# First output product of a two-layer encoder: the loads of the last two gates on ScalarE's queue, and the residual of one quarter loaded into its row tile ahead

## The chip, the cores and the metric

The kernel runs on one core of one Trainium2 chip. The metric is the time of one execution on the device in microseconds (us), taken as the median of several runs.

A core has five engines that each work through their own instructions in order: TensorE (PE, matrix products), VectorE (DVE), ScalarE (ACT), GpSimd (POOL) and SyncE (SP). They wait for one another through semaphores. SP issues most DMA transfers; POOL issues some, among them all that add to what is in the target (accumulate); ScalarE issues one small one at the start and six stores of the output at the end.

## The reference

Two encoder layers over `x` (512 tokens x 1024) and 256 memory tokens. Each layer projects its normed input to mixer heads, memory queries and a gate, and ends with a gated output projection that is added to the residual:

```python
for i in range(DEPTH):                    # DEPTH = 2
    h = rmsnorm(x, norm_g[i])
    mem_h = rmsnorm(mem, mem_norm_g[i])
    proj = jnp.einsum('bsd,de->bse', h, w_in)          # w_in_a in layer 0, w_in_b in layer 1
    ...                                                # split into mixer heads, q_mem and gate
    o = concat(mixer(...), memory_attention(q_mem, mem_h, ...))   # 512 x 1536: 8 mixer heads, 4 memory heads
    x = x + (o * silu(gate)) @ w_out[i]                # w_out: 1536 x 1024
```

The part that matters here is the last line in the first layer (called layer A below).

## The kernel before

**Products.** Every projection is computed in float32 by splitting both factors into a high and a low part and adding three products: high x high (`mm_early`, L177), low activation x high weight (L178) and high activation x low weight (`mm_late`, L181). On top of that, large products are taken as 2 x 2 blocks with seven block products instead of eight (the Strassen-Winograd scheme). The block products are called 11, 12, S1, S2, S3, S4 and 22; the four quarters of the result are called 11, 12, 21 and 22, where the first digit is the half of the tokens (rows) and the second the half of the output columns.

**Weights.** One weight tile is 128 x 1024 (512 KB). SP loads it (`wl`, L259), ScalarE rounds it to the high part (`wh`, L321), DVE subtracts for the low part (`wo`, L331). Some tiles are sums of weight blocks that POOL's accumulating DMAs build (L295, L305). TensorE uses one tile in one "run" of eight early and four late matmuls of 128 x 512.

**Order.** The program is written out in Python and nothing reorders it later. A `Driver` counts slots (one per run): generators such as `fold` or `gate.ev` do one step in a slot and `yield n` to come back n slots later. So the text of a step, its yields and the slot in which it started decide where its instructions stand in each engine's order.

**Gates of layer A.** The last chunks of layer A are `b`, `m` and `a` (`A_ORDER = "01234567bma"`): the gates of heads 4 to 7 (g = 2), of the memory heads (g = 0) and of heads 0 to 3 (g = 1). `gate.ev` takes a quarter of a gate's product, `load()` fetches the head outputs `od` from DRAM into a tile `og` (256 KB, L863, on SP), ScalarE takes tanh (L886), DVE makes the SiLU and multiplies by `og` (L878) into `yf`. `prep_y` makes the seven activation blocks `YW` from `yf` (casts L919, subtractions L920, differences such as L942 and L947), `prep_l` those of gate `b`, called `YL` (L994, L997).

**Output product.** `out_proj` calls `s_chunk` with `late=YL`. The seven block products come in the order `PRODUCTS_3` (11, S3, 12, S1, S2, S4, 22), each in three runs, the third with `YL`. Behind each stands one step of `after`, done for each of two token rows `u`: hold z, hold s3, add_11, hold s5, fold s2, add 12, add 21. The pieces of the result lie in four "row tiles" `acc` (128 tokens x 1024 each; rows 0 and 1 hold the quarters 11 and 12, rows 2 and 3 the quarters 21 and 22); `place(q, u)` gives the half of a row tile that belongs to quarter q. `fold` forms t3 + b and t5 - (t3 + b), where b is the S2 product in PSUM.

**Residual and norm.** `x` is added by an accumulating DMA of POOL into the finished quarter: in `ev_all` (L1081) for rows 0 and 1, in `ahead` (L1089) for rows 2 and 3 before their last addition. When both halves of a row are done, `ev_o` stores it (`x1d`, SP L1574) and norms it for the next layer: squares on ScalarE (L559), `rstd` on POOL (L561, L519, L520), the multiply on DVE (L566), then transposes on TensorE (`xT`, L572) in `first_t` and `diffs_t`, which split them into `h` and differences `f`. Meanwhile TensorE takes eight runs on the normed memory tokens (`act`).

Of the kernel before, what the change touches and what calls it, by code (L numbers as in the profile page):

```python
# [13 lines left out]
ALU = mybir.AluOpType  # L14
# [118 lines left out]
def trunk_kernel(ctx: ExitStack, tc: tile.TileContext, x, mem, wall, norm_g, mem_norm_g, gcol,  # L133
                 qn_a, kn_a, qn_b, kn_b, ident_d, mask_d, tab_a, tab_b, out):
    nc = tc.nc
    V, A, G, T = nc.vector, nc.scalar, nc.gpsimd, nc.tensor
# [11 lines left out]
    def m4(dt=F32, name="m4"):  # L148
        return pool.tile([128, 1024], dt, tag="m4", name=name, bufs=NM4)
# [240 lines left out]
    def s_chunk(n, act, ev, tokens=True, pre=None, half=False, soon=False, tight=False, place=None, pairs=False, K=4, tail=None, turn=None, late=None, ahead=None):  # L390
# [17 lines left out]
        def diff(u):  # L408

            if (u, "22") not in snap:  # L410
                c = snap[u, "22"] = snap["s5", u]
                V.tensor_tensor(c, c, snap["s3", u], ALU.subtract)  # L412

        def add(q, name, u, b):
            t = snap[name, u]
            if name == "s3" and late is None:
                diff(u)
            if tail and q == "11":
                yield from tail[3](u, t, b)
                return  # L420
            t_, b_ = turn(t, b) if turn else (t, b)
            V.tensor_tensor(t_, b_, t_, ALU.subtract if q == "12" else ALU.add)  # L422
            if not tail:
                yield 1
            yield from ev(q, u, t)

        def hold(name, u, b):
            t = snap[name, u] = place({"z": "11", "s3": "21", "s5": "22"}[name], u)
            A.copy(t, b)
            yield 1  # L430
            if name == "s5":
                ahead("22", u, t)
# [9 lines left out]
        def fold(name, u, b):  # L442
            t, t3, t5 = place("12", u), snap["s3", u], snap["s5", u]
            snap[name, u] = t
            A.copy(t, b)
            yield 1
            G.dma_start(t3, t, accum_op=ALU.add)
            yield 2
            V.tensor_tensor(t5, t5, t3, ALU.subtract)
            ahead("21", u, t3)  # L450
            yield 1
            yield from ev("22", u, t5)
# [6 lines left out]
        for i, (a, s, fresh) in enumerate(order):  # L459
# [4 lines left out]
            for x in range(runs):  # L464
# [11 lines left out]
                if tail and i > 4:  # L476
                    if i == 5:
                        drv.free()
                    for b in range(2):
                        o, ts = bank[s][b], slice(b * 128, (b + 1) * 128)  # L480
# [362 lines left out]
    def gates(od, o_done, o_here, direct, fused=False, turn=None):  # L843
# [3 lines left out]
        def gate(H, first, g, half=False):  # L847


            if g < 2:  # L850
                yf[g] = [m4(name="yf") for _ in range(2)]

            def ev(q, u, t):
                i, j = int(q[0]) - 1, int(q[1]) - 1
                h0, ts = first + 2 * j, slice(i * 256, (i + 1) * 256)
                hs, got, asked = (h0, h0 + 1), {}, []
                tv = t.rearrange("p (h t) -> p h t", h=2)

                def load():
                    if "o" not in got and all(h in o_done for h in hs):  # L860
                        asked.append(h0)
                        o = got["o"] = s2(name="og")
                        nc.sync.dma_start(o.rearrange("p (h t) -> p h t", h=2), od[h0:h0 + 2, :, ts].rearrange("h p t -> p h t"))  # L863
                        got[h0] = got[h0 + 1] = o.rearrange("p (h t) -> p h t", h=2)
                    for n, h in enumerate(hs):
                        if h in got:
                            continue
                        if h in o_here:
                            got[h] = o_here[h][:, None, ts].to_broadcast([128, 2, 256])
                        elif h in o_done and (hs[1 - n] in direct):  # L870
                            o = s2(name="og")[:, 0:256]
                            nc.sync.dma_start(o, od[h, :, ts])
                            asked.append(h)
                            got[h] = o[:, None, :].to_broadcast([128, 2, 256])

                def times(dst):
                    if "o" in got:
                        V.tensor_tensor(dst, t, got["o"], ALU.mult)  # L878
                    else:
                        dv = dst.rearrange("p (h t) -> p h t", h=2)  # L880
                        for n, h in enumerate(hs):
                            V.tensor_tensor(dv[:, n], tv[:, n], got[h][:, n], ALU.mult)

                load()
                th = s2(name="th")
                A.activation(th, t, AF.Tanh, scale=0.5)  # L886
                yield 1
                V.scalar_tensor_tensor(t, th, 1.0, t, ALU.add, ALU.mult)
                yield 1
                if not all(h in got for h in hs):  # L890
                    load()
                    while not all(h in got for h in hs):
                        yield 1
                        asked.clear()
                        load()
                    if asked:
                        yield 1
                if g < 2:
                    times(yf[g][j][:, i * 512:(i + 1) * 512])
                    y_done.add((g, i, j))  # L900
                    return
                times(t)
                yield 1
                ys[2 * j + i] = t

            s_chunk(256, H, ev, tokens=False, half=half, soon=g == 2, turn=turn)
# [152 lines left out]
    def out_proj(YW, ys, src, evac, tiles, half=False, last=None):  # L1059

        acc, done = {}, set()

        def place(q, u):
            i = int(q[0]) - 1
            if 2 * i not in acc:
                for v, t in enumerate(tiles()):
                    acc[2 * i + v] = halves(t)
            return acc[2 * i + u][int(q[1]) - 1]

        def ev(q, u, t):  # L1070
            b, n = 2 * (int(q[0]) - 1) + u, int(q[1]) - 1
            G.dma_start(t, src[b][:, n * 512:(n + 1) * 512], accum_op=ALU.add)
            yield 2
            done.add((n, b))

        prep_l, YL = ys

        def ev_all(q, u, t):
            b, n = 2 * (int(q[0]) - 1) + u, int(q[1]) - 1
            if not b // 2:  # L1080
                G.dma_start(t, src[b][:, n * 512:(n + 1) * 512], accum_op=ALU.add)  # L1081
                yield 2
            done.add((n, b))
            if {(0, b), (1, b)} <= done:
                yield from evac(n, b, acc[b])

        def ahead(q, u, t):
            b, n = 2 + u, int(q[1]) - 1
            G.dma_start(t, src[b][:, n * 512:(n + 1) * 512], accum_op=ALU.add)  # L1089

        if not last:
            s_chunk(512, YW, ev_all, half=half, tight=True, place=place, late=YL, ahead=ahead)
            return
        drv.spawn(prep_l())
        s_chunk(512, YW, ev, half=half, tight=True, place=place)

        def ev_l(q, u, t):
            b, n = 2 * (int(q[0]) - 1) + u, int(q[1]) - 1
            while (n, b) not in done:
                yield 1  # L1100
            V.tensor_tensor(acc[b][n], t, acc[b][n], ALU.add)
            yield from evac(n, b, acc[b])

        def sum_11(u, z, p):
            t = s2(name="sn")
            A.copy(t, p)
            yield 1
            G.dma_start(acc[u][0], t, accum_op=ALU.add)
            yield 1
            yield from evac(0, u, acc[u])  # L1110

        def sum_kept(name, u, t):
            b, n = (u, 0) if name == "z" else (2 + u, 1)
            assert (n, b) in done
            if name == "z":
                G.dma_start(acc[b][n], t, accum_op=ALU.add)
            else:
                V.tensor_tensor(t, t, acc[b][n], ALU.add)

        def sum_22(u, t, p):  # L1120
            V.tensor_tensor(t, t, p, ALU.subtract)
            last(1, 2 + u, t, slice(0, 512), nc.sync)

        def sum_21(u, _, p):
            assert (0, 2 + u) in done
            t = acc[2 + u][0]
            for c, queue in ((slice(0, 256), nc.scalar), (slice(256, 512), nc.sync)) if u else ((slice(0, 512), nc.scalar),):
                V.tensor_tensor(t[:, c], p[:, c], t[:, c], ALU.add)
                last(0, 2 + u, t, c, queue)

        s_chunk(512, YL, ev_l, tight=True, K=2, tail=(sum_kept, sum_22, sum_21, sum_11))
# [118 lines left out]
    p = turn4(mg[0, 0], None, None)  # L1250
# [13 lines left out]
    def ahead(u, b):  # L1264

        if (u, b) == (0, 0):
            place_m(1, 0)
            W.hi(True)
            W.hi(True)
        if (u, b) == (0, 1):  # L1270
            place_m(0, 1)
            place_m(1, 1)
# [28 lines left out]
    od = dram.tile([12, 128, S], F32, name="od", bufs=1)  # L1301
# [603 lines left out]
```

## Time and profile before

| what | value |
|---|---|
| median of 3 runs | 958.94 us (958.92 to 960.17) |
| profiled execution | 960.2 us |
| its span in the profile | 958.4 us |
| TensorE busy | 935.0 us (98%), 5456 matmuls |
| DVE busy | 799.3 us (83%) |
| ScalarE busy | 696.7 us (73%) |
| POOL busy | 360.9 us (38%) |

The profile is one execution. Times in its lists are from the start of the span; a matmul's end is modelled, so neighbouring matmuls overlap in the records. Windows give busy time per engine, and `PEclk` the mean clock that was granted to TensorE (1.00 is full). In a timeline row the bracket at the end gives the idle time of that engine ahead of the instruction and what ended it. "DMA to landing" is the time from issue until the data are there. In the chain of waits each row is the piece of work that the next one waited for.

### The profile page before, as it was taken

The numbers are of one execution on the slowest core, as the hardware profiler recorded it, in microseconds if no ns is written. First come the engines' busy times: TensorE is split into PE (matmuls) and PEld (weight loads), VectorE is DVE, ScalarE is ACT, GpSimd is POOL, SyncE is SP. The second block draws the span as 40 slices with busy tenths as digits, with TensorE's granted clock in tenths as the row PEclk, the third lists the DMA queues.
The fourth block names the chain that finished last, engine by engine and source line by source line (L and its number), as shares of the span: only waits on it lengthen the run. The fifth ranks groups of instructions, "written<-read, shape, count | busy, mean of one in ns | idle before, by whom it ended". The sixth has DMA issues, their size and how long they took to land. (4 is left out here: it accounts for less than half of the span.)

```text
span 958.4 us, 16243 instructions
## 1 busy us (share of the span) xinstructions
PE 935.0 (98%) x5456; PEld 817.6 (85%) x5456; DVE 799.3 (83%) x1440; ACT 696.7 (73%) x1728; POOL 360.9 (38%) x506
## 2 busy tenths in 40 slices
PE   8999999999999999999999997988999999999998
PEld 6889888888888888888899995766988999999886
DVE  6998678879797979798889896857798998779977
ACT  7775788777777777777676674636778887778774
POOL 3411424565565555556543111216252431011122
PEclk9999999999999999999999998997999999999999
DMA  9999949976868687776859999989985586776777
GB/s 348 387 259 333 280 108 254 307 169 191 209 202 223 196 209 209 191 227 165 233 147 293 214 286 259 271 219 303 296 203 124 149 239 169 183 216 134 196 175 177
DMA packets 85517, 214.49 MB, mean 224 GB/s; under 512 B 19129, under 2 KB 28857, under 8 KB 85434
## 3 DMA queue, kind: packets, MB, share of 16 engines
q1 hardware_dynamic: 63466, 143.78, 42.3%
q0 software_dynamic: 20960, 68.17, 38.3%
q10 hardware_dynamic: 1008, 1.51, 0.4%
q8 instruction: 43, 0.70, 0.3%
q14 instruction: 40, 0.33, 0.1%
HBM read 163.55 MB, written 13.17 MB: 184 GB/s over the span
## 5 line engine op out<-in xcount | busy, mean ns | idle before, releaser
L331 DVE TENSOR_TENSOR wo<-wl,wh 128x1024 fp32r<-128x1024 f32 x261 | 319.6, 1229 | 10.2 <-ACT wh L321 9.9
L321 ACT CAST wh<-wl 128x1024 fp32r<-128x1024 f32 x261 | 275.3, 1060 | 27.0 <-PE pj L178 16.5
L177 PE MATMUL pj<-wh,hS 128*128 128x512 f32 (+1 forms) x416 | 154.4, 380 | 0.0
L178 PE MATMUL pj<-wh,hS 128*128 128x512 f32 (+1 forms) x416 | 149.1, 367 | 0.4 <-DVE hS L651 0.4
L177 PE MATMUL pj<-wh,h 128*128 128x512 f32 (+1 forms) x312 | 115.2, 378 | 0.0
L178 PE MATMUL pj<-wh,h 128*128 128x512 f32 (+1 forms) x312 | 111.6, 367 | 0.0
L520 POOL TENSOR_TENSOR rstd<-mse,half 128x4 f32<-128x4 f32 (+2 forms) x98 | 101.8, 1039 | 8.2
L181 PE MATMUL pj<-wo,hS 128*128 128x512 f32 (+1 forms) x416 | 99.5, 366 | 0.0
L178 PEld LDWEIGHTS pj<-wh,hS 128*128 128x128 f32 x416 | 78.7, 189 | 11.9 <-DVE hS L651 0.6
L177 PEld LDWEIGHTS pj<-wh,hS 128*128 128x128 f32 x416 | 78.6, 189 | 10.9
L519 POOL TENSOR_SCALAR mse<-hss 128x4 f32<-128x4 f32 (+1 forms) x88 | 45.8, 521 | 109.9 <-ACT junk L675 102.3
L181 PEld LDWEIGHTS pj<-wo,hS 128*128 128x128 f32 x416 | 72.5, 189 | 13.1
L675 ACT ACTIVATE junk<-sn 128x128 f32<-128x128 f32 x264 | 79.3, 310 | 2.2 <-DVE sn L412 2.2
L1360 POOL TENSOR_TENSOR ta<-sn,tabs 128x128 f32<-128x128 f32 (+1 forms) x64 | 38.3, 606 | 108.5 <-DVE sn L680 84.9
L399 ACT COPY sn<-pj 128x512 f32<-128x512 f32 x122 | 67.3, 590 | 14.0 <-PE pj L181 12.8
L259 POOL DMA_DIRECT2D wl<-in_wall_dram x44 | 41.8, 999 | 94.5 <-PE pt L1507 25.2
L181 PE MATMUL pj<-wo,h 128*128 128x512 f32 (+1 forms) x312 | 74.5, 365 | 0.0
L305 POOL DMA_DIRECT2D wl<-wl x35 | 31.4, 905 | 102.1 <-DVE wo L331 60.6
L422 DVE TENSOR_TENSOR sn<-pj,sn 128x512 f32<-128x512 f32 x89 | 60.8, 684 | 6.9 <-PE pj L181 6.6
L178 PEld LDWEIGHTS pj<-wh,h 128*128 128x128 f32 x312 | 59.0, 189 | 8.3
L177 PEld LDWEIGHTS pj<-wh,h 128*128 128x128 f32 x312 | 59.0, 189 | 8.2
L295 POOL DMA_DIRECT2D wl<-wl x35 | 32.9, 974 | 87.6 <-DMA wl<-in_wall_dram 16.1
(292 smaller groups left out, 2395.7 us busy)
## 6 DMA issues: line engine op xcount, KB each, us to landing
wl<-in_wall_dram SPq DMA_DIRECT2D x226, 512.0 KB, 7.4
wl<-wl POOLq DMA_DIRECT2D x70, 512.0 KB, 6.4
wl<-in_wall_dram POOLq DMA_DIRECT2D x48, 512.0 KB, 8.6
od<-o SPq DMA_DIRECT2D x11, 256.0 KB, 3.8
og<-od SPq DMA_DIRECT2D x10, 256.0 KB, 7.8
x<-in_x_dram SPq DMA_DIRECT2D x4, 512.0 KB, 8.8
v0r<-sn SPq DMA_DIRECT2D x8, 256.0 KB, 10.7
v0d<-v0r SPq DMA_DIRECT2D x4, 512.0 KB
```

The source lines that it names most:

```text
L177: T.matmul(o, a, b, start=start, stop=False, skip_group_check=True)
L178: T.matmul(o, c, d, start=False, stop=False, skip_group_check=True)
L181: T.matmul(o, a, b, start=False, stop=stop, skip_group_check=True)
L259: queue.dma_start(t, wall[d], **how)
L321: A.copy(wh, self.tile[self.items[i]])
L331: V.tensor_tensor(wo, self.tile[key], wh.bitcast(F32), ALU.subtract)
L399: A.copy(t_, b_)
L422: V.tensor_tensor(t_, b_, t_, ALU.subtract if q == "12" else ALU.add)
L519: G.tensor_scalar(e, ss, EPS, None, ALU.add)
L520: G.tensor_tensor(r, e, half[:, 0:n], ALU.pow)
L675: A.activation(jk, p[:, j * 128:(j + 1) * 128], AF.Square, scale=by, accum_out=ss[:, j:j + 1])
L1360: G.tensor_tensor(ta[:, 0:n], xn[:, 0:n, 0:32], ropeA[:, 0, b, s0:s0 + n], ALU.mult)
```

## The change

Three edits. The `og` loads of the gates `m` and `a` (the fused layer A, g < 2) are issued by ScalarE on its own queue instead of by SP; the gate `b` and layer B stay on SP. The step `hold z` now also has SP load `x` of quarter 12, plainly, into that quarter's half of the row tile. `fold` drops ScalarE's copies, POOL's accumulating transfer from tile to tile and a yield of two slots; in their place DVE adds the S2 product to t3 straight from PSUM and subtracts it from the preloaded residual. Signs follow: add 12 becomes an addition in this product. The residual accumulate of quarter 12 in `ev_all`, and its two-slot yield, go.

```diff
-            V.tensor_tensor(t_, b_, t_, ALU.subtract if q == "12" else ALU.add)
+            V.tensor_tensor(t_, b_, t_, ALU.subtract if q == "12" and late is None else ALU.add)
...
         def hold(name, u, b):
             t = snap[name, u] = place({"z": "11", "s3": "21", "s5": "22"}[name], u)
             A.copy(t, b)
+            if name == "z":
+                ahead("12", u, place("12", u))
             yield 1
...
         def fold(name, u, b):
             t, t3, t5 = place("12", u), snap["s3", u], snap["s5", u]
             snap[name, u] = t
-            A.copy(t, b)
-            yield 1
-            G.dma_start(t3, t, accum_op=ALU.add)
-            yield 2
+            V.tensor_tensor(t3, t3, b, ALU.add)
+            V.tensor_tensor(t, t, b, ALU.subtract)
+            yield 1
             V.tensor_tensor(t5, t5, t3, ALU.subtract)
             ahead("21", u, t3)
...
-                        nc.sync.dma_start(o.rearrange("p (h t) -> p h t", h=2), od[h0:h0 + 2, :, ts].rearrange("h p t -> p h t"))
+                        (nc.scalar if fused and g < 2 else nc.sync).dma_start(o.rearrange("p (h t) -> p h t", h=2), od[h0:h0 + 2, :, ts].rearrange("h p t -> p h t"))
...
         def ev_all(q, u, t):
             b, n = 2 * (int(q[0]) - 1) + u, int(q[1]) - 1
-            if not b // 2:
+            if q == "11":
                 G.dma_start(t, src[b][:, n * 512:(n + 1) * 512], accum_op=ALU.add)
                 yield 2
...
         def ahead(q, u, t):
-            b, n = 2 + u, int(q[1]) - 1
-            G.dma_start(t, src[b][:, n * 512:(n + 1) * 512], accum_op=ALU.add)
+            b, n = 2 * (int(q[0]) - 1) + u, int(q[1]) - 1
+            if q == "12":
+                nc.sync.dma_start(t, src[b][:, n * 512:(n + 1) * 512])
+            else:
+                G.dma_start(t, src[b][:, n * 512:(n + 1) * 512], accum_op=ALU.add)
```

The edits move instructions. The line numbers after the change are 1 to 4 higher. The first place is ScalarE's order at the end of gate `a`, where the last two `og` loads now stand; before:

```order
L165 CAST pT<-pt 128x512 x2
L321 CAST wh<-wl 128x1024
L886 ACTIVATE th<-sn 128x512
L1538 COPY o<-oo 128x512
L321 CAST wh<-wl 128x1024
L919 CAST y_7242<-yf 128x512 x2
L886 ACTIVATE th<-sn 128x512
L429 COPY acc<-pj 128x512 x2
L321 CAST wh<-wl 128x1024 x3
```

and now:

```order
L321 CAST wh<-wl 128x1024
L864 DMA og<-od 128x2x256
L887 ACTIVATE th<-sn 128x512
L1542 COPY o<-oo 128x512
L321 CAST wh<-wl 128x1024
L920 CAST y_7242<-yf 128x512 x2
L864 DMA og<-od 128x2x256
L887 ACTIVATE th<-sn 128x512
L429 COPY acc<-pj 128x512 x2
L321 CAST wh<-wl 128x1024 x3
```

Each load stands right ahead of its gate's tanh, the last one behind the two casts of L919 (now L920); the rest of ScalarE's order there is as it was.

The second place is DVE's order from the end of the S2 product on (`m` are the memory tokens, `act` their transposed and split form, `acc` the row tiles); before:

```order
L331 TENSOR_TENSOR wo<-wl,wh 128x1024 x3
L566 SCALAR_TENSOR_TENSOR m<-m,rm,row 128x512 x2
L422 TENSOR_TENSOR acc<-pj,acc 128x512 x2
L331 TENSOR_TENSOR wo<-wl,wh 128x1024
L566 SCALAR_TENSOR_TENSOR m<-m,rm,row 128x512 x2
L168 TENSOR_TENSOR act<-xT,act 128x4x128 x2
L449 TENSOR_TENSOR acc<-acc 128x512 x2
L331 TENSOR_TENSOR wo<-wl,wh 128x1024
L168 TENSOR_TENSOR act<-xT,act 128x4x128 x2
L331 TENSOR_TENSOR wo<-wl,wh 128x1024
L422 TENSOR_TENSOR acc<-pj,acc 128x512 x2
L331 TENSOR_TENSOR wo<-wl,wh 128x1024 x4
```

and now:

```order
L447 TENSOR_TENSOR acc<-acc,pj 128x512
L448 TENSOR_TENSOR acc<-acc,pj 128x512
L447 TENSOR_TENSOR acc<-acc,pj 128x512
L448 TENSOR_TENSOR acc<-acc,pj 128x512
L331 TENSOR_TENSOR wo<-wl,wh 128x1024 x2
L450 TENSOR_TENSOR acc<-acc 128x512 x2
L331 TENSOR_TENSOR wo<-wl,wh 128x1024
L567 SCALAR_TENSOR_TENSOR m<-m,rm,row 128x512 x2
L422 TENSOR_TENSOR acc<-pj,acc 128x512 x2
L331 TENSOR_TENSOR wo<-wl,wh 128x1024
L567 SCALAR_TENSOR_TENSOR m<-m,rm,row 128x512 x2
L168 TENSOR_TENSOR act<-xT,act 128x4x128 x2
```

The four new operations stand at the start; the pair that forms t5 (L449, now L450) moves from behind both halves of the memory tokens' norm to two weight tiles behind them.

The third place is POOL's order in the same stretch (`sn` is the tile of add_11); before:

```order
L305 DMA wl<-wl 128x1024 x3
L438 DMA acc<-sn 128x512 x2
L1081 DMA acc<-in_x_dram 128x512 x2
L1089 DMA acc<-in_x_dram 128x512 x2
L447 DMA acc<-acc 128x512 x2
L1089 DMA acc<-in_x_dram 128x512 x2
L1081 DMA acc<-in_x_dram 128x512 x2
L561 TENSOR_TENSOR mse<-ss 128x1
```

and now:

```order
L305 DMA wl<-wl 128x1024 x3
L440 DMA acc<-sn 128x512 x2
L1082 DMA acc<-in_x_dram 128x512 x2
L1093 DMA acc<-in_x_dram 128x512 x4
L562 TENSOR_TENSOR mse<-ss 128x1
```

The transfer from tile to tile and the accumulate of quarter 12 are gone, and the two residuals of quarter 21 follow those of quarter 22 directly.

Three shifts follow from the shorter waits. On TensorE the first 16 transposes of the row tiles stand behind the third run of `act` instead of the fifth; the second 16 stay behind the sixth. On DVE four of the eight norm multiplies of the row tiles stand three weight tiles earlier than the other four. On SP the two loads of `x` stand among the weight loads at the start of the output product, and the stores of x1d for rows 0 and 1 stand five weight loads earlier.

## Prediction

> **What bounds the kernel now.** I read the page's totals first, then windows of busy time around the edit, then TensorE's waits in that stretch, the chain of waits through it, and last the timeline and the DMA landings at the two places where the chain leaves TensorE.
>
> ```profile
> span 958.4 us, 16243 instructions
> PE 935.0 (98%) x5456; PEld 817.6 (85%) x5456; DVE 799.3 (83%) x1440; ACT 696.7 (73%) x1728; POOL 360.9 (38%) x506
> ```
>
> TensorE is the bound: 935.0 of 958.4 us. So the change can gain only where TensorE idles or runs at a lower granted clock, and every other microsecond on DVE, ScalarE or POOL is worth nothing by itself. The windows show where that is. Columns: length; busy time and count of PE, PEld, DVE, ACT, POOL; granted clock; DMA share; GB/s.
>
> ```profile
> 500.00:560.00 60.00, 60.00 (x501) 59.81 (x501) 54.70 (x114) 40.97 (x77) 15.19 (x20) 1.00 0.97 259
> 585.00:600.00 15.00, 8.64 (x27) 5.66 (x25) 12.73 (x20) 5.54 (x9) 3.24 (x4) 0.77 0.98 249
> 600.00:635.00 35.00, 34.67 (x160) 28.64 (x161) 26.26 (x33) 21.26 (x30) 8.16 (x10) 1.00 0.91 264
> 635.00:651.00 16.00, 12.84 (x49) 9.59 (x48) 9.29 (x12) 7.09 (x18) 7.31 (x10) 0.89 0.90 227
> 651.00:675.00 24.00, 19.42 (x94) 16.08 (x93) 18.50 (x27) 15.92 (x39) 12.88 (x16) 0.86 1.04 308
> 675.00:700.00 25.00, 24.58 (x189) 23.61 (x188) 20.95 (x27) 18.33 (x41) 5.68 (x7) 1.00 1.05 285
> 700.00:958.00 258.00, 253.08 (x1672) 230.13 (x1670) 224.06 (x375) 199.80 (x451) 64.42 (x71) 1.00 0.71 177
> ```
>
> Two holes stand around the first output product: 6.4 us idle in 585 to 600, and 7.7 us idle in 635 to 675 (3.16 + 4.58), both with the granted clock down at 0.77 to 0.89. Between them and behind them TensorE is full. What it waits for there, and the chain through both holes:
>
> ```profile
> PE xT L572 <- ACT f L633: 4.6, 2, 3.4
> PE pj L181 <- DVE wo L331: 4.4, 3, 2.6
> PE pj L177 <- ACT yl L994: 2.5, 1, 2.5
> PE pj L178 <- DVE yl L997: 2.1, 1, 2.1
> ...
> 570.21 16.55 DMA og<-od
> ...
> 605.14 0.91 PE pj L181 x4
> 607.86 0.91 PE pj L181 x4
> ...
> 616.51 1.08 ACT acc L445 x2
> 617.58 8.31 DMA acc<-acc
> ```
>
> The names in the waits (ScalarE, DVE) are the last link only. The chain says what made DVE late: the last `og` load, 16.55 us, and then the fold's transfer. One run (one weight tile) takes 607.86 - 605.14 = 2.72 us when nothing is late.
>
> **First part: the og loads on ScalarE's queue.**
>
> ```profile
> 570.21 0.38 SPq L863 DMA_DIRECT2D og<-od  x1
> 571.71 1.13 ACT L919 CAST y<-yf 128x512 fp32r<-128x512 f32 x2
> 574.77 1.21 DVE L331 TENSOR_TENSOR wo<-wl,wh 128x1024 fp32r<-128x1024 f32 x1
> 580.48 0.69 DVE L878 TENSOR_TENSOR yf<-sn,og 128x512 f32<-128x512 f32 x1 [4.50 <-DMA og<-od]
> 582.52 0.50 PE L177 MATMUL pj<-wh,y 128*128 128x512 f32 x1 [0.22 <-ACT acc L429]
> 586.86 0.69 DVE L878 TENSOR_TENSOR yf<-sn,og 128x512 f32<-128x512 f32 x1 [3.95 <-DMA og<-od]
> 600.28 0.50 PE L177 MATMUL pj<-wh,yS 128*128 128x512 f32 x1 [0.66 <-ACT sn L436]
> ...
> acc<-sn POOLq DMA_DIRECT2D x2, 256.0 KB, 7.6
> og<-od SPq DMA_DIRECT2D x2, 128.0 KB, 3.2
> ...
> q0 software_dynamic: 627, 2.24, 70.3%
> q1 hardware_dynamic: 928, 1.96, 34.5%
> ```
>
> DVE, which works in order, sits 4.50 and 3.95 us in front of the last two gate products (L878). From the last of them, 586.86, to the S1 product's first matmul, 600.28, lie 13.4 us of DVE and ScalarE work (window 585 to 600: DVE 12.73 of 15). I take these to shift as a block.
>
> The last load now stands on ScalarE behind the casts of L919, which end at 572.84, against an issue at 570.21 on SP: it is issued 2.6 us later. It must land sooner by more than that to gain. How long it takes alone on a queue of its own the trace doesn't show at this place. Bounds: 3.2 us (half of the bytes, on SP, at a calmer moment) and 16.55 us (the same load here). Nearest is a transfer of the same 256 KB that POOL issued soon after, with weight loads of SP's queue beside it (`acc<-sn`, in the DMA view of 600 to 602): 7.6. I take 7.5, so it lands at about 580.4, 6.4 us before 586.86. DVE's part follows: the third load is then landed when DVE is done with the wo that ends at 575.98, so nothing else of the 8.5 us of waiting is in the way. Could TensorE use 6.4 us? The middle product's three runs end at the earliest at 582.52 + 3 x 2.72 = 590.7, and S1 would start at 593.9, so yes, with about 3 us of waiting left over. That leftover still breaks TensorE's work, and I allow 1.0 us for a lowered clock behind it (the window's 0.77 over 8.64 us busy cost some 2 us). Gain: 5.4 us.
>
> ```profile
> L1789 ACTq DMA_DIRECT2D out_dram<-acc x4: 338/346/473, 949.7 to 953.7; - x4
> SPq L863 <- DMA od<-o: 4.0, 1, 4.0
> ```
>
> The cost of issuing: 8 DMAs by 0.35 us from the only issues that ScalarE has now, 2.8 us. In 500 to 560 ScalarE has 19 us idle, so I cost this at nothing; without that cover it would come to 2.8 us at most. New waits: each load waits on ScalarE for its heads' `od` to be stored, and behind it stand its own tanh and the next weight cast (L321), for which DVE's subtraction and then TensorE wait. On SP the trace has one such wait on `od`, of 4.0 us. SP loses eight issues and these waits, so weight loads come no later.
>
> The Trainium skill, page "DMA: Bandwidth & Descriptors", section "Issuing engines are not separate DMA queues", says that DMAs started by ScalarE, SP or GpSimd run on the same 16 engines and interleave, so that spreading them saves only the issue. By that sentence alone the load would take its 16.55 us again, and this part would lose time. The same page, "Queues, rings and completion order", says that each engine takes turns between the queues that have work; by that a lone load passes the weight loads queued ahead on SP. The trace can't show which: between 570 and 586 only POOL's queue (q0, 70.3% of the engines' time) and SP's (q1, 34.5%) had work.
>
> **Second part: the fold and the residual.**
>
> ```profile
> 632.87 1.28 DVE L449 TENSOR_TENSOR acc<-acc 128x512 f32<-128x512 f32 x2
> 635.14 0.39 PE L177 MATMUL pj<-wh,act 128*128 128x512 f32 x1
> 642.44 0.69 DVE L422 TENSOR_TENSOR acc<-pj,acc 128x512 f32<-128x512 f32 x1 [4.82 <-DMA acc<-in_x_dram]
> 645.00 0.63 ACT L559 ACTIVATE sq<-acc 128x512 f32<-128x512 f32 x1 [8.90 <-DMA acc<-in_x_dram]
> 654.19 1.91 PE L572 MATMUL xT<-ident,acc 128*128 128x128 f32 x16
> 655.64 1.41 DVE L566 SCALAR_TENSOR_TENSOR acc<-acc,rstd,row 128x512 f32<-128x512 f32 x2 [0.46 <-POOL rstd L520]
> 664.66 1.97 PE L572 MATMUL xT<-ident,acc 128*128 128x128 f32 x8 [1.18 <-ACT f L633]
> 673.69 0.28 PE L177 MATMUL pj<-wh,h 128*128 128x256 f32 x1
> ...
> acc<-in_x_dram POOLq DMA_DIRECT2D x2, 256.0 KB, 8.8
> ```
>
> What the hole is worth: eight runs of `act` (the memory tokens' projection) and 32 transposes stand between 635.14 and 673.69. At full rate they take 8 x 2.72 + 2 x 1.91 = 25.6 us. They took 38.55. So 13.0 us are lost, waiting and lowered clock together: the most that this part can give.
>
> How it arises: the S2 product ends at 616.5, the copies take 1.08, the transfer from tile to tile 8.31, then DVE's subtraction L449 waits for its turn until 632.87 and only at 634.15 may POOL add the residual to the last quarter. That lands at 642.4, the final sums, norms (squares from 645.00, last norm multiply to 657.05, 12.05 us in all) and transposes follow.
>
> After: behind S2's end four DVE operations of 0.69 (2.8), two wo of 1.21 (2.4) that stand between in the order, and the pair L449 of 1.28: 616.5 + 6.5 = 623.0. POOL's residual load, 8.8, lands at 631.8. The quarter's product ends at 635.1, so the transfer is hidden with 3.3 us to spare, and the sum L422 runs at 635.1 instead of 642.44. The second quarter has its residual already in the row tile, so rows 0 and 1 are complete when S4 has ended (600.28 + 9 x 2.72 = 624.8). Their squares need ScalarE only, and by 643.3 (the end of three `act` runs), where the first 16 transposes now stand, there are 18 us for what took 12.05 for all four. Rows 2 and 3 are complete at 636.5; with the whole 12.05 us behind that they are normed at 648.6, and the second 16 transposes are due at 635.14 + 6 x 2.72 + 1.91 = 653.4: 4.8 us to spare.
>
> Costs: DVE gets four operations and loses none, 2.8 us, in a stretch where it has 8.7 of 35 idle; TensorE's margin there is the wo of the next run. If that cover is gone the four cost 2.8. ScalarE loses 1.08 us of copies. POOL loses four accumulates. SP's two plain loads stand in its order right at the first product's end, three products ahead of the fold (9 runs, 24 us); at nothing, and if they were late the fold would wait for them (rival 4). The stores of x1d on SP, now ahead of five more weight loads, wait for the sums only, which come earlier than before. Transposes and copies of the earlier norm now share DVE's and ScalarE's time with weight preparation: I allow 2 of the 13.0 us for that. Gain: 11.0 us.
>
> **What follows.** Behind 675 TensorE has 24.58 of 25 and 253.08 of 258 us, so the shift is carried to the end.
>
> Sum: 5.4 + 11.0 = 16.4. The profiled execution has a span of 958.4 and a time of 960.2; the median of the runs is 958.94, and I take the sum from that: 942.5 us.
>
> **Rivals.**
> 1. The load lands no sooner on its own queue: 572.84 + 16.55 = 589.4, 2.5 us later than now. The DMA share of 0.98 to 1.05 speaks for it: the engines have no room. Against it, the 7.6 us of POOL's transfer in the same stretch. The Trainium skill's first sentence above would have it so. Then 958.9 + 2.5 - 11.0 = 950.4.
> 2. The second hole finds its next wait: DVE is busy 18.50 of 24 in 651 to 675, and the norm, the copies and the wo tiles are squeezed into fewer microseconds. With half of the 13.0 gained, 6.5 instead of 11.0, the time is 4.5 more: 947.0.
> 3. Slower: ScalarE, in order, stands still at the og loads. Eight waits of 4.0 and 2.8 for issuing make 34.8 us against 19 idle, 16 too much; spread over the casts that feed TensorE, 16 more than before, which with a gain of 16.4 is about level, and with the loads landing no sooner (2.5 + 16 - 11) is 7.5 slower: 966. It decides from about 11 us of standstill on. Against it: on SP only one such wait was found, of 4.0 us, and one alone falls into ScalarE's idle time.
> 4. The residual load of the second quarter is late or is held on SP: the fold waits, and the second hole stays. 958.9 - 5.4 = 953.5.
>
> **Chances and range.** Forecast 0.62; rival 1 0.13, rival 2 0.15, rival 3 0.05 (half of that at about level or faster), rival 4 0.05. Low end: a landing of 3.2 (576.0; DVE itself then allows 8.5 us, but TensorE's 590.7 lets through all of it) and the whole 13.0: 958.9 - 8.5 - 13.0 = 937.4. High end: rival 1, 951. The forecast's own range is 938 to 946. 0.2% (1.9 us) is about what a measurement of this kernel can tell from no change: faster 0.94, within it 0.02, slower 0.04.
>
> **What would show it.** Right: og rows on ScalarE's queue with landings of 5 to 9 us; no idle time in front of L878 over 1 us; the S1 product starting near 594; the pair of subtractions L450 some 6 us behind S2's end; the waits of the transposes and of L181 gone, the granted clock near 1.00 through the second hole, and its eight runs and 32 transposes done in 26 to 29 us. Wrong: landings of 12 us or more, ScalarE idle in front of a tanh with TensorE waiting for a wh or wo between 480 and 575, or transposes that still wait for the norms or for copies of xT.

## The result, and the profile after

The changed kernel takes 949.31 us (median of 4 runs, 948.45 to 950.61), against 959.56 for the kernel before in the same comparison: a ratio of 0.9892 (95% interval 0.9871 to 0.9912). That is 10.2 us faster; 16.4 were forecast (942.5 us). The range of 937 to 951 held it near its upper end, which was that of rival 1; the forecast's own range of 938 to 946 did not.

The page's head of the changed kernel, and its windows in the same columns as before:

```profile
span 948.8 us, 16240 instructions
...
585.00:600.00 15.00, 7.15 (x22) 4.88 (x23) 10.82 (x18) 3.03 (x5) 2.61 (x3) 0.78 1.06 263
600.00:635.00 35.00, 35.00 (x156) 28.61 (x156) 30.46 (x40) 20.45 (x29) 7.03 (x8) 0.95 0.92 256
635.00:651.00 16.00, 16.00 (x81) 13.51 (x80) 14.04 (x19) 13.55 (x30) 7.79 (x13) 1.00 1.00 350
651.00:675.00 24.00, 22.66 (x150) 20.59 (x150) 20.93 (x28) 18.17 (x40) 9.55 (x9) 1.00 1.03 266
```

The second hole is closed: TensorE has 16.00 of 16 and 22.66 of 24 us where it had 12.84 and 19.42, at full clock. The first hole is still there, and wider in this execution: 7.15 of 15 where it had 8.64.

TensorE's waits from 560 to 680, the piece of the chain at the first hole, and the timeline at the marks of the prediction:

```profile
PE pj L181 <- DVE wo L331: 3.6, 2, 3.0
PE pj L177 <- ACT yl L995: 2.5, 1, 2.5
PE pj L178 <- DVE yl L998: 2.1, 1, 2.1
PE pj L177 <- ACT kmT L725: 1.3, 1, 1.3
...
560.82 12.79 DMA og<-od
...
574.57 14.70 DMA og<-od
...
573.64 0.69 DVE L879 TENSOR_TENSOR yf<-sn,og 128x512 f32<-128x512 f32 x1 [4.04 <-DMA og<-od]
582.75 0.69 DVE L879 TENSOR_TENSOR yf<-sn,og 128x512 f32<-128x512 f32 x1 [2.62 <-DMA og<-od]
589.36 0.69 DVE L879 TENSOR_TENSOR yf<-sn,og 128x512 f32<-128x512 f32 x1 [4.18 <-DMA og<-od]
602.80 0.79 PE L177 MATMUL pj<-wh,yS 128*128 128x512 f32 x1
619.35 0.69 DVE L447 TENSOR_TENSOR acc<-acc,pj 128x512 f32<-128x512 f32 x1 [0.69 <-PE pj L181]
624.24 0.69 DVE L450 TENSOR_TENSOR acc<-acc 128x512 f32<-128x512 f32 x1
637.72 0.39 PE L177 MATMUL pj<-wh,act 128*128 128x512 f32 x1
663.01 0.28 PE L177 MATMUL pj<-wh,h 128*128 128x256 f32 x1
```

The last og load is issued at 574.57 on ScalarE's queue and takes 14.70 us, hardly less than the 16.55 on SP. It lands at 589.27, so the last gate product stands at 589.36 (before: 586.86) and the S1 product starts at 602.80 (before: 600.28): in this execution the first part cost 2.5 us. From the first `act` run to the first run on `h` it takes 663.01 - 637.72 = 25.3 us, where it took 38.55: the second part gave 13.3. The waits of the transposes (L572, now L573) are gone. A wait of 1.3 us is new, in front of the second run on `hS` (673.59), for a copy of the memory keys (`kmT`, L725). Sum: -2.5 + 13.3 - 1.3 = 9.5; the spans differ by 958.4 - 948.8 = 9.6.

So the open question was the first part: why a queue of its own didn't bring the load sooner.

### The profile page after: what moved, and what is told of

It reads as the page before. It is cut to its first block, busy times and chain, and to the rows that moved or that the text cites. A ratio compares the mean times of both kernels' runs of the same rounds, so it can differ in the third digit from the quotient of the medians.

```text
span 948.8 us, 16240 instructions
## 1 busy us (share of the span) xinstructions
PE 931.3 (98%) x5456; PEld 816.2 (86%) x5456; DVE 801.5 (84%) x1444; ACT 695.3 (73%) x1726; POOL 355.4 (37%) x502
## 4 chain that ended last, share of the span: by engine, by line
PE 86%; DVE 6%; ACT 4%; DMA 3%; issue 1%; POOL 0%; DVEq 0%; ACTq 0%; POOLq 0%
PE pj L178 22%; PE pj L177 22%; PE pj L181 22%; DMA og<-od 3%; PE qT L688 3%; DVE wo L331 2%; PE sa L1423 2%; PE ptb L1738 1%; PE oo L1532 1%; PE sa L1419 1%; PE pt L1511 1%; PE xT L573 1%; ACT wh L321 1%; PE ob L181 1%; PE ob L178 1%
## 5 line engine op out<-in xcount | busy, mean ns | idle before, releaser
L422 DVE TENSOR_TENSOR sn<-pj,sn 128x512 f32<-128x512 f32 x89 | 60.8, 684 | 7.0 <-PE pj L181 6.6
```

The costliest lines, as they stand in the source:

```text
L422: V.tensor_tensor(t_, b_, t_, ALU.subtract if q == "12" and late is None else ALU.add)
```

## The experiments

**Each part alone.** First the queue alone:

```diff
-                        nc.sync.dma_start(o.rearrange("p (h t) -> p h t", h=2), od[h0:h0 + 2, :, ts].rearrange("h p t -> p h t"))
+                        (nc.scalar if fused and g < 2 else nc.sync).dma_start(o.rearrange("p (h t) -> p h t", h=2), od[h0:h0 + 2, :, ts].rearrange("h p t -> p h t"))
```

> The kernel before, with only the og loads of gates m and a moved to ScalarE's queue. Theory A (the 16 DMA engines take turns by packet between the queues, so the load of 1 KB packets lands no sooner and starts later): the last gate product of DVE near 589.4 instead of 586.86, the S1 product near 602.9 instead of 600.28, and the 2.5 us carried to the end: about 961.5 us, ratio 1.0026. Theory B (the own queue brings the load sooner, and the changed kernel lost it by something in its second part): about 953.5 us, ratio 0.994.

Measured: 961.04 us against 959.92, ratio 1.0016 (1.0005 to 1.0027). A small loss, on theory A's side; theory B is out. The places that theory A named are not borne out by the profiled execution (959.37 us, among the shorter of its 11):

```profile
570.93 0.37 ACTq L863 DMA_DIRECT2D og<-od  x1
572.21 1.14 ACT L919 CAST y<-yf 128x512 fp32r<-128x512 f32 x2
586.85 0.69 DVE L878 TENSOR_TENSOR yf<-sn,og 128x512 f32<-128x512 f32 x1 [4.95 <-DMA og<-od]
```

The last load is issued 0.7 us later than on SP and 1.3 us ahead of the casts behind which it stands in the program's order. It lands in time for a gate product at 586.85, and the S1 product starts at 600.28, both as before (589.4 and 602.9 were expected). So the load came no sooner, but the 2.5 us of the changed kernel's profile are not a fixed price; where this run's 1.5 us go isn't shown.

Then the second part alone, the changed kernel with that line put back:

```diff
-                        (nc.scalar if fused and g < 2 else nc.sync).dma_start(...)
+                        nc.sync.dma_start(...)
```

> The changed kernel with the og loads back on SP; fold and preloaded residual stay. Theory A: 2.6 us better than the changed kernel, about 946.7 us, ratio 0.987 to the kernel before; eight act runs and 32 transposes in 26 to 28 us. Theory B: worse than the changed kernel by the 5.4 us forecast for the queue, about 954.5 us.

Measured: 948.52 us, ratio 0.9879 (0.9865 to 0.9894). That is theory A's side again, though the queue costs less than the 2.6 us that were expected: its own ratio says 1.5 us, and the two versions of the second part, 0.9892 and 0.9879, overlap in their intervals. The whole gain of the change is the second part.

**Why the load is slow on its own queue.** The DMA view of the changed kernel between 570 and 574, when three queues have work (q0 is POOL's, q1 SP's, q10 ScalarE's; columns: packets, MB, share of the 16 engines' time):

```profile
q0 software_dynamic: 139, 0.50, 63.1%
q1 hardware_dynamic: 139, 0.51, 33.7%
q10 hardware_dynamic: 139, 0.13, 9.4%
```

Each queue moves the same number of packets, 139. A packet of q10 has 1 KB (0.13 MB by 139), since an og load takes two heads' 256 tokens from a layout by head; the packets of the others have 3.6 KB. So the queue gets a third of the turns and a ninth of the bytes. From 574 to 578 and from 578 to 582 the counts are equal again (137 to 138 and 154 to 156). The Trainium skill's page "DMA: Bandwidth & Descriptors", section "Queues, rings and completion order", says that each engine takes turns between queues packet by packet; the equal counts agree.

At 139 packets in 4 us a load's 256 packets need some 7.4 us (an estimate). The 14.70 us are longer because the last load was not alone on its queue: the one ahead, issued at 565.54, held its gate product until 582.75, and the last product followed 6.6 us behind (589.36). In the runs with the queue alone and with 1 KB packets and a preload (below) the last load took 15.83 and 14.81 us.

The test is to double the packet: `od` is laid out by gate quarter, so that a load is 128 packets of 2 KB.

```diff
-    od = dram.tile([12, 128, S], F32, name="od", bufs=1)
+    od = dram.tile([6, 2, 128, S], F32, name="od", bufs=1)
...
-        nc.sync.dma_start(od[i], t)
+        for n in range(2):
+            nc.sync.dma_start(od[i // 2, n, :, (i % 2) * 256:(i % 2) * 256 + 256], t[:, n * 256:n * 256 + 256])
...
-(nc.scalar if fused and g < 2 else nc.sync).dma_start(o.rearrange("p (h t) -> p h t", h=2), od[h0:h0 + 2, :, ts].rearrange("h p t -> p h t"))
+(nc.scalar if fused and g < 2 else nc.sync).dma_start(*((o, od[h0 // 2, i]) if fused else (...)))
```

> The changed kernel (og on ScalarE's queue), with od laid out in DRAM by gate quarter, so that an og load is 128 packets of 2 KB instead of 256 of 1 KB. Theory A, turns by packet: in 570 to 590 each queue moved 34 to 42 packets per us, so a load needs some 3.5 us of turns and about 2 us around them; the last one issued near 574.6 lands near 580.5 instead of 589.3, and the time falls by 7 to 8 us to about 942 us, ratio 0.982. Theory C (bytes or a fixed latency of the own queue decide, not packets): the landing stays near 589 and the time at 949.3.

Measured: 948.45 us, ratio 0.9879 (0.9865 to 0.9892). The landing came as theory A said, the time didn't. DVE's and POOL's rows and TensorE's wait in that run:

```profile
570.77 0.34 ACTq L864 DMA_DIRECT2D og<-od  x1
580.63 0.69 DVE L879 TENSOR_TENSOR yf<-sn,og 128x512 f32<-128x512 f32 x1 [1.96 <-DMA og<-od]
594.06 0.50 PE L177 MATMUL pj<-wh,yS 128*128 128x512 f32 x1 [2.12 <-ACT sn L438]
607.54 0.87 POOL L1082 DMA_DIRECT2D acc<-in_x_dram  x1 [10.90 <-DMA acc<-sn]
610.67 2.15 POOL L1093 DMA_DIRECT2D acc<-in_x_dram  x2
620.62 0.69 DVE L450 TENSOR_TENSOR acc<-acc 128x512 f32<-128x512 f32 x1 [5.56 <-DMA acc<-in_x_dram]
...
600.00:635.00 35.00, 30.82 (x134) 25.42 (x133) 24.37 (x33) 15.81 (x26) 5.28 (x6) 0.90 1.00 288
...
PE xT L573 <- issue: 4.2, 1, 4.2
```

The S1 product starts at 594.06, 8.7 us earlier than in the changed kernel. Then the fold's subtraction L450 stands 5.56 us in DVE's order, because quarter 22 has to have its residual first: POOL had waited 10.90 us for add_11's transfer before it could issue that load at 610.67. Behind L450 stands the norm of the memory tokens, so TensorE has no transposes to do (the profile names no releaser for this wait), idles 4.2 us and runs at 0.90 over 30.82 us, by estimate another 3.1. Of 8.7 us about 7.3 are given back.

The same layout with the loads on SP:

```diff
-(nc.scalar if fused and g < 2 else nc.sync).dma_start(*(...))
+nc.sync.dma_start(*(...))
```

> The same layout of od with the og loads on SP. Theory A: behind weight loads on one queue the last load waits for all packets ahead of it; two loads have 256 packets fewer, at some 37 packets per us that is 6.9 us: landing near 580 instead of 586.8, time about 940 to 942 us, ratio 0.981. Theory C: as the second part alone, 946.7 us.

Measured: 947.78 us, ratio 0.9863 (0.9843 to 0.9882). No clear gain over the second part alone: theory A's count of packets ahead was wrong for SP. The profiled execution is the fastest of the four, 943.79 us against 947.69 to 948.14 for the others:

```profile
582.97 0.69 DVE L879 TENSOR_TENSOR yf<-sn,og 128x512 f32<-128x512 f32 x1 [2.58 <-DMA og<-od]
```

There the load, issued at 569.85, took 13.0 us, at least 3.5 less than in the other profiles with SP's queue (16.55 before), so its time on SP differs between executions. Why isn't shown.

**Taking the next wait away.** The residual of quarter 22 is loaded ahead by SP too, and DVE adds the product to it:

```diff
-            A.copy(t, b)
-            if name == "z":
-                ahead("12", u, place("12", u))
+            if name == "s5":
+                V.tensor_tensor(t, t, b, ALU.add)
+            else:
+                A.copy(t, b)
+                q = {"z": "12", "s3": "22"}[name]
+                ahead(q, u, place(q, u))
             yield 1
-            if name == "s5":
-                ahead("22", u, t)
...
-            if q == "12":
+            if q in ("12", "22"):
                 nc.sync.dma_start(t, src[b][:, n * 512:(n + 1) * 512])
```

It was put on three versions: 2 KB packets on ScalarE's queue, 2 KB packets on SP, and the changed kernel itself (1 KB packets on ScalarE's queue).

> The kernel with 2 KB packets of od on ScalarE's queue, and in addition the residual of quarter 22 loaded ahead by SP (the product added by DVE), in place of ScalarE's copy and POOL's accumulate. Theory A with a next wait: the last og load did land near 580 and the S1 product started near 594, but DVE's subtraction waited 5.6 us for POOL's residual of quarter 22, and TensorE lost 4.2 us at the memory tokens' transposes and some 3 at a lowered clock. Without that wait the time is 8 us under the changed kernel, 941 us, ratio 0.981. Rival (the early S1 product is given back elsewhere, by weight tiles or by the clock): 946 to 949 us.

> The same residual of quarter 22 ahead, with the 2 KB og loads on SP. Theory A with a next wait: the S1 product starts near 596.4 (last gate product at 583), every execution like the fastest one of the kernel without this edit: 943 us, ratio 0.983, about 2 us behind the same on ScalarE's queue. Rival: 946 to 948 us.

> The changed kernel (og on ScalarE's queue in 1 KB packets) with the residual of quarter 22 loaded ahead. Theory A with a next wait: the last og load still lands near 587 to 589, so the preload finds nothing to free: 948 to 950 us, ratio 0.989. Rival (the preload of quarter 22 alone made the 941.5 us): 941 to 944 us.

| version with the residual of 22 ahead | median, us | ratio to before (95%) | last gate product starts |
|---|---|---|---|
| 2 KB packets, ScalarE's queue | 941.54 | 0.9815 (0.9801 to 0.9828) | 580.44 |
| 2 KB packets, SP's queue | 947.82 | 0.9882 (0.9868 to 0.9895) | 586.45 |
| 1 KB packets, ScalarE's queue | 947.60 | 0.9882 (0.9863 to 0.9902) | 585.47 |

The first came out as theory A had it (941); for SP the rival did (946 to 948). On top of the second part (948.52), neither the own queue nor the longer packets alone, nor any two of own queue, longer packets and preload, bring a clear gain; all three bring some 7 us. The preload alone, with 1 KB packets on SP, was not run. The third version came out just under theory A's 948 to 950, well short of the rival's 941 to 944. DMA view of 570 to 574, then chain and timeline rows of the first version, and last a chain row of the second:

```profile
q0 software_dynamic: 131, 0.47, 59.0%
q1 hardware_dynamic: 126, 0.47, 31.1%
q10 hardware_dynamic: 125, 0.25, 16.3%
...
570.82 9.53 DMA og<-od
...
614.78 1.29 DVE L451 TENSOR_TENSOR acc<-acc 128x512 f32<-128x512 f32 x2
593.87 0.50 PE L177 MATMUL pj<-wh,yS 128*128 128x512 f32 x1 [2.14 <-ACT sn L439]
628.47 0.39 PE L177 MATMUL pj<-wh,act 128*128 128x512 f32 x1
600.00:635.00 35.00, 35.00 (x164) 29.19 (x163) 32.02 (x43) 20.47 (x33) 7.91 (x11) 1.00 1.05 357
```

```profile
569.53 16.83 DMA og<-od
```

Turns are still about equal (131, 126, 125) and q10's bytes have doubled (0.25 MB for 0.13). The load takes 9.53 us, the subtraction L451 waits for nothing, and TensorE is full at full clock from 600 to 635. On SP the same load, issued 1.3 us earlier, takes 16.83 in the profiled execution (13.0 in that of the run without the preload): it stays behind the weight loads issued ahead of it on that queue, and by the medians halving the packets of a load that waits in line changes little. The first version beats both kernels.

**What held the second hole.** The fold alone, with the late residual kept:

```diff
             A.copy(t, b)
+            V.tensor_tensor(t3, t3, b, ALU.add)
             yield 1
-            G.dma_start(t3, t, accum_op=ALU.add)
-            yield 2
             V.tensor_tensor(t5, t5, t3, ALU.subtract)
```

> The kernel before, with only the fold on DVE (t3 plus the product straight from PSUM); ScalarE's copy into quarter 12 and POOL's late residual for it stay. Theory D (the transfer from tile to tile alone held the stretch: DVE stood in front of it, and the residual transfers behind it): the subtractions L448 some 6 us after the S2 product, the late residual of quarter 12 lands near 633, all eight norm multiplies done by 646, the first transposes stand behind the fifth act run (649): the waits of the transposes go and the time is that of the whole second part, 948 to 949.5 us, ratio 0.988. Theory E (the late residual of quarter 12 held half of it): 952 to 955 us.

Measured: 948.20 us, ratio 0.9883 (0.9870 to 0.9897), the whole gain of the second part. Its stretch from the first `act` run to the first run on `h` takes 26.7 us (634.95 to 661.68), 1.4 more than the changed kernel's, with a wait of the transposes:

```profile
PE xT L571 <- ACT f L632: 1.0, 1, 1.0
```

The wait for `kmT` is absent here, so by these traces that wait takes back what the residual ahead gains in the stretch. And the residual ahead alone, with the transfer kept (the second part's kernel, its fold changed):

```diff
-            V.tensor_tensor(t3, t3, b, ALU.add)
+            c = s2(name="sn")
+            A.copy(c, b)
             V.tensor_tensor(t, t, b, ALU.subtract)
             yield 1
+            G.dma_start(t3, c, accum_op=ALU.add)
+            yield 2
```

> The kernel before, with the residual of quarter 12 loaded ahead, but the fold still by a copy (into a tile of its own) and POOL's transfer. Theory D: the transfer, 8 to 10 us from 617, still makes the subtraction and the last residual of quarter 21 late (landing near 639 to 640), and rows 2 and 3 are normed only near 652, about when the second transposes are due: some of the gain stays out, 950 to 953 us. Theory E: about half of the gain, 953 to 954 us. If neither the transfer nor the late residual alone is enough to stop TensorE, both this and the DVE fold alone come to 948 to 949.5.

Measured: 954.54 us, ratio 0.9942 (0.9930 to 0.9954). Timeline rows, a wait and a window of this run:

```profile
618.41 1.76 POOL L451 DMA_DIRECT2D acc<-sn  x2 [4.46 <-ACT sn L448]
630.94 1.28 DVE L453 TENSOR_TENSOR acc<-acc 128x512 f32<-128x512 f32 x2
639.77 0.69 DVE L422 TENSOR_TENSOR acc<-pj,acc 128x512 f32<-128x512 f32 x1 [4.01 <-DMA acc<-in_x_dram]
...
647.79 1.22 PE L181 MATMUL pj<-wo,act 128*128 128x512 f32 x2 [3.05 <-DVE wo L331]
...
PE pj L181 <- DVE wo L331: 6.0, 4, 3.1
...
635.00:651.00 16.00, 12.06 (x51) 9.59 (x50) 9.81 (x12) 8.55 (x19) 10.94 (x13) 0.88 1.04 321
```

The transfer makes the subtraction late (630.94), that makes the residual of quarter 21 late, and DVE stands 4.01 us at L422 with weight tiles behind it. Of TensorE's 6.0 us of waiting for weight tiles, 3.9 lie here (12.06 busy of 16, at a clock of 0.88) and the rest in the first hole. So the transfer from tile to tile was what held the hole, and with it gone the residual of quarter 12 ahead gains nothing more: the fold on DVE alone gives all, the preload alone about half. Theory D named the mechanism and was low on this run's time by some 1.5 us; the 953 to 954 of theory E is nearer here, but its 952 to 955 for the fold alone is out.

## Why the prediction was right or wrong

- **The bound and the two holes** were read rightly: what TensorE gained lies in the second hole, what it lost in the first and in the 1.3 us behind.
- **The landing of the og load** is the step that failed. I took 7.5 us between 3.2 and 16.55; it was 14.70. The row that I called nearest, POOL's `acc<-sn` at 7.6, was of the same bytes but not of the same packets, nor in the same traffic: it was issued at 600, behind the crowded stretch, and its rows are 2 KB long. I had the shares of the two queues quoted and didn't work out what a third one with 1 KB packets would get. With three queues it gets a ninth of some 280 GB/s. One load by itself would still need only some 7.4 us by the packet counts (6.6 lie between the last two gate products): the 7.5 was about right, by luck of the row, for a load alone on the queue. What it left out is the og load ahead, which was still on the queue when the last one was issued. The 13.4 us behind the last gate product held (602.80 - 589.36), and with 2 KB packets and the preload the forecast's places came: a landing at 580.4 and the S1 product at 593.87.
- **The issue** was later than forecast too, 574.57 for 572.84, because the load issued at 560.82 took 12.79 us and held the gate product of 573.64, for which ScalarE stood 6.54 us in front of a copy (L1542); the load was issued right behind that copy's start. The reason that I gave, that the load has to wait for the casts in front of it, was wrong: it was issued 1.3 us ahead of them, and in the four other profiles with ScalarE's queue at 570.57 to 570.93, hardly later than on SP.
- **Rival 1** came true in its result: it gave 950.4 us and a landing at 589.4; measured 949.31 and 589.27. It had 0.13. That the landing fits so well is partly luck: the issue was 1.7 us later than it had it and the load 1.85 us shorter, and in the other two profiles with 1 KB packets on this queue it landed at 586.8 and 585.4. By the sentence on the Trainium skill's page "DMA: Bandwidth & Descriptors", section "Issuing engines are not separate DMA queues", this was the outcome, and the queue alone agrees (1.0016); the version at 941.54 doesn't, since there the own queue brings the load 6 us sooner than SP with the same packets (2.5 us against the fastest execution on SP).
- **The cost of issuing and ScalarE's waits** (rival 3) were right at nothing up to 560: TensorE has 60.00 of 60 us in 500 to 560 in the changed kernel too. Behind that, ScalarE stood 6.54 us once for a gate product whose og load was late (2.41 at that place before).
- **The second part** was right in its mechanism, step by step: L450 at 624.24, 4.9 us behind the first of the four new operations (619.35), the residuals hidden, the transposes without waits. SP's two plain loads had more than the 24 us that I gave them: they were issued by 574, 45 us ahead of the fold. Its size was 13.3, not 11.0: the 2 us that I kept for DVE were not needed there. The forecast gave the residual ahead a share in it; the fold alone brings the same time.
- **Carried to the end**: all but 1.3 us, a new wait for `kmT` (rival 2 in small).

## What to carry to other kernels

Where the DMA engines are full, a transfer moved to another queue got an equal number of packets here, not of bytes: look at the packet counts and bytes per queue in that stretch, lengthen the moved transfer's rows (here from 1 to 2 KB) before expecting it sooner, and count the loads already on the new queue. A product in PSUM (128 x 512) that must be added to a tile cost DVE 0.69 us here, and 8.3 us and a copy as an accumulating transfer, with whatever stands behind it in order. When an early stage is made faster, look for the transfer further on whose slack it eats: here about 7.3 of 8.7 us went back into a residual that had been early enough until then.

## What the runs showed of the hardware

Three queues with work moved 139, 139 and 139 packets in 4 us, though the packets of two had 3.6 KB and those of the third 1 KB; doubling one queue's packet from 1 to 2 KB doubled its bytes (0.13 to 0.25 MB) at nearly the same number of turns (125). A load of 256 KB on ScalarE's own queue, with another og load ahead of it, then took 9.53 and 9.77 us in two runs, for 14.70 to 15.83 in three runs with 1 KB; on SP, in line behind weight loads, it took 16.83 and, in the fastest execution, 13.0. A load on ScalarE's queue was issued 1.3 us before casts began that stand ahead of it in the program's order.
